# Moving four low-part subtractions to GpSimd, and a sum of the input's blocks behind the last attention unit

## The chip, the cores and the metric

The kernel runs on one core of a Trainium2 chip. Its engines are TensorE (PE: matmuls and transposes, with PEld for its weight loads), VectorE (DVE), ScalarE (ACT), GpSimd (POOL) and SyncE (SP), which issues the transfers. The metric is the time of one execution in microseconds of device time; the median of three runs stands for a kernel.

## The reference

One layer of a decoder over 512 positions of width 1024: a normalisation, one input projection, three attention branches (A block-sparse, B dilated in three groups, C sliding-window with sinks), each times a SiLU gate, a merge with sigmoid gates, and an output projection. Cut to what matters here:

```
hn = rms_norm(x, ln_g)
proj = hn @ w_in                       # q, k, v and silu inputs of A, B, C; gate logits
o_a, o_b, o_c = moba(...), dilated(...), swa_sink(...)
branches = stack([o_a * silu(ga), o_b * silu(gb), o_c * silu(gc)])
br = einsum('bsiw,iwd->bsid', branches, w_branch)
gates = sigmoid(gate_logits.reshape(b, s, 3, 1024))
merged = sum(gates * br, axis=2)
x = x + merged @ w_out
```

## The kernel before

**Precision.** Every large product is made of three: each operand is split into a high part of reduced precision and a low part, what is left of it. A weight tile w of 128 x 1024 is loaded by DMA; ScalarE casts it to whi (`split_hi`, L135); wlo = w − whi is a subtraction on VectorE or on GpSimd (`split_lo`, L140). In `load_w` (from L153) a counter sends every `every`-th of these to GpSimd and the others to VectorE, so `every=1` means all on GpSimd, and 1000 none. The same `split_lo` makes the low parts of softmax weights (ptlo), of row factors (ws) and of branches (bp) on VectorE.

**Stages.** Attention runs in ten units in turn, A0, W0, R0, Z0, A1, W1, R1, Z1, C0 and C1: A is branch A, W, R and Z are the three groups of branch B, and C0 and C1 are the two halves of branch C, four heads each. In a C unit, TensorE makes scores (L723 and L724), VectorE's row operation adds the bias and takes the row's extremum (`softmax_rows`, L584; it reads the scores from PSUM), ScalarE takes the exponential (L585), TensorE transposes (L731) and multiplies by the values (L610). When a unit ends, its row sums are inverted (L988 to L991 for C; L1018 to L1024 for B, where three groups are merged), and `spread` turns the factors into a row layout: a cast (L820), a subtraction ws (L140), transposes on TensorE (L827), a copy (L829), and a product that broadcasts them (L835), by which VectorE multiplies the output (L992, L1028).

**Filler.** The gates behind attention are a list of jobs. Jobs 0 and 1 ("raw", the SiLU inputs of B and A) are plain products of hn with weight tiles (L281 to L283); TensorE does them between the steps of C0 and C1, where it would wait for row operations. Their eight weight tiles are w_5105 to w_5147 (steps of 6) in the order's numbering. Job 2 ("gl", the first sigmoid gate, tiles w_5506 to w_5524) is plain too. From job 3 on the products use seven block products in place of eight, for which the input's blocks have to be added and subtracted first: `fast_x`, whose sums xf (L325) and differences (L339 to L346) run on VectorE. Behind C1 follow, for each gate, a load of the weights, sums of the weights' blocks, and the products.

**What sets the order.** Each engine works through a fixed order of its own. The kernel is traced in program order, and a scheduler with a model of the timeline then places each instruction; `tc.issue_after(x)` keeps what is issued within it behind instruction x. `fast_x()` was called without one: its inputs, the parts xhi and xlo of hn, are ready early, and each of its sums could go into any gap of VectorE once its buffer was free.

Of the kernel before, what the change touches and what calls it, by code (L numbers as in the profile page):

```python
# [12 lines left out]
ALU = mybir.AluOpType  # L13
# [7 lines left out]
KT = 8  # L21
# [82 lines left out]
def body(tc, x, ln_g, w_in, qk_g, sinks, w_branch, w_out, rel_bias, c_ident, c_onehot, c_mask, c_expand, out):  # L104
    nc = tc.nc
    V, A, G, T = nc.vector, nc.scalar, nc.gpsimd, nc.tensor
# [7 lines left out]
    with top:  # L114
# [18 lines left out]
        def split_hi(dst, src, eng=A):  # L133
            if eng is A:
                A.copy(dst, src)  # L135
            else:
                eng.tensor_copy(dst, src)  # L137

        def split_lo(dst, src, hi, eng=V):
            eng.tensor_tensor(dst, src, hi.bitcast(F32), ALU.subtract)  # L140
# [12 lines left out]
        def load_w(pieces, kts, early=False, every=LOEVERY):  # L153


            ncol = sum(n for n, _ in pieces)
            per = 1024 // ncol
            his, los = [], []
            for k0 in range(0, kts, per):
                w = wp.tile([128, per, ncol], F32, name="w32", tag="w32", bufs=LBUFS)  # L160
                o = 0
                for n, src in pieces:
                    nc.sync.dma_start(w[:, :, o : o + n], src(k0, k0 + per))
                    o += n
                hi = wp.tile([128, per, ncol], F32R, name="whi", tag="whi")
                lo = wp.tile([128, per, ncol], F32R, name="wlo", tag="wlo")
                nw[0] += 1
                split_hi(hi, w, V if early and nw[0] % 2 else A)
                split_lo(lo, w, hi, G if nw[0] % (2 if early else every) == 0 else V)
                his.append(hi)  # L170
                los.append(lo)
            return (lambda k: his[k // per][:, k % per]), (lambda k: los[k // per][:, k % per])

        def win_piece(c, n):
            return (n, lambda k0, k1: win[:, k0:k1, c : c + n])
# [100 lines left out]
        def gate_cols(w, c, psum):  # L276

            whi, wlo = w
            for k in range(KT):
                a = whi(k)[:, c : c + 128]  # L280
                T.matmul(psum, a, xhi[:, k, :], start=(k == 0), stop=False)  # L281
                T.matmul(psum, a, xlo[:, k, :], start=False, stop=False)  # L282
                T.matmul(psum, wlo(k)[:, c : c + 128], xhi[:, k, :], start=False, stop=(k == KT - 1))  # L283
                yield
# [32 lines left out]
        def fast_x():  # L317

            def quarter(k, j):
                ks, js = slice(4 * k, 4 * k + 4), slice(256 * j, 256 * j + 256)  # L320
                return xhi[:, ks, js], xlo[:, ks, js]

            def full(dst, k, j, eng):
                h, l = quarter(k, j)
                eng.tensor_tensor(dst, h.bitcast(F32), l.bitcast(F32), ALU.add)  # L325

            def parts(w, nm, eng):
                hi = gp.tile([128, 4, 256], F32R, name=nm + "h", tag=nm + "h", bufs=1)
                lo = gp.tile([128, 4, 256], F32R, name=nm + "l", tag=nm + "l", bufs=1)
                split_hi(hi, w)  # L330
                split_lo(lo, w, hi, eng)
                return hi, lo

            X, Y = (qkv.tile([128, 4, 256], F32, name="xf", tag="qlo") for _ in range(2))
            Z = gp.tile([128, 4, 256], F32, name="xf", tag="sm", bufs=1)
            full(X, 0, 1, V)
            full(Y, 0, 0, V)
            full(Z, 1, 1, V)
            V.tensor_tensor(Y, X, Y, ALU.subtract)  # L339
            t1 = parts(Y, "t1", V)  # L340
            V.tensor_tensor(X, Z, X, ALU.subtract)
            t3 = quarter(0, 1)
            V.tensor_tensor(Z, Z, Y, ALU.subtract)
            t2 = parts(Z, "t2", V)
            full(Y, 1, 0, V)
            V.tensor_tensor(Y, Y, Z, ALU.subtract)  # L346
            t4 = parts(Y, "t4", V)
            split_hi(t3[0], X)
            split_lo(t3[1], X, t3[0])
            return [quarter(0, 0), t1, t2, quarter(1, 0), t3, t4, quarter(1, 1)]  # L350
# [62 lines left out]
        def job_load(n):  # L413
            if n >= len(jobs):
                return None
            ty, u, v = jobs[n]
            if ty in ("raw", "gl"):
                c0 = v if ty == "raw" else GL + v * D + u * 512
                if n < PLAIN:
                    return load_w([win_piece(c0, 512)], KT, every=2)  # L420
                return fast_weights(lambda i, k: win[:, 4 * k : 4 * k + 4, c0 + 256 * i : c0 + 256 * i + 256])
            if ty == "br":
                return load_w([(512, lambda k0, k1: wbr[v, :, k0:k1, u * 512 : u * 512 + 512])], 4, every=1000)
            return load_w([(1024, lambda k0, k1: wou[:, k0:k1, :])], KT, every=1000)
# [3 lines left out]
        def raw_tile(br, hf):  # L428
            raws[br, hf] = qkv.tile([128, 2, S], F32, name="graw", tag=tags_raw[br, hf])
            return raws[br, hf]  # L430
# [14 lines left out]
        with att:  # L445
# [132 lines left out]
                v = tl[:, c0 : c0 + 128]  # L578
                return bass.AP(v.tensor, v.offset, [list(v.ap[0]), [step, n], [1, 128]])

            last_exp = [None]

            def softmax_rows(lg, sc, bt, init, mcol, lcol):
                V.tensor_tensor_reduce(lg, sc, bt, 1.0, init, ALU.add, ALU.min, mcol)  # L584
                last_exp[0] = A.activation(lg, lg, AF.Exp, bias=mcol, scale=-1.0, accum_out=lcol)  # L585

            def take_transposed(pend, tr):
# [453 lines left out]
        def slot(nm, tag, dt=F32R):  # L1041
            if tag[0] == "t":
                return gp.tile([128, 2, S], dt, name=nm, tag=tag, bufs=1)
            return qkv.tile([128, 2, S], dt, name=nm, tag=tag, **({"bufs": ORAWS} if tag == "oraw" else {}))
# [20 lines left out]
        xs = None  # L1065
# [12 lines left out]
        for n in range(2, len(jobs) - 1):  # L1078
            ty, dh, i = jobs[n]
            if n == PLAIN:  # L1080
                xs = fast_x()
            w, wnext = wnext, job_load(n + 1)
            if ty == "raw":
                fast_cols(w, xs, [raw_tile(dh, hf) for hf in range(2)], keep)
            elif ty == "gl":
                br = "ABC"[i]
                if dh == 0:
                    silu(br)
                sgs = [gp.tile([128, 2, S], F32, name="gsg", tag="sg") for _ in range(2)]
                if n < PLAIN:  # L1090
                    for dc in range(4):
                        pj = ps.tile([128, 512], F32, name="pj", tag="pj")
                        for _ in gate_cols(w, dc * 128, pj):
                            pass
                        A.activation(sgs[dc // 2][:, dc % 2], pj, AF.Sigmoid)
                else:
                    fast_cols(w, xs, sgs, gate)
            else:
                br = "ABC"[i]
                for dc in range(4):  # L1100
                    tg = ("pj", "sc", "tr", "po")[dc]
                    po = gsc[0][:, 1] if tg == "sc" else ps.tile([128, 512], F32, name="po", tag=tg)
                    for k in range(4):
                        a = w[0](k)[:, dc * 128 : dc * 128 + 128]
                        bh, bl = bhi[i, k // 2][:, k % 2], blo[i, k // 2][:, k % 2]
                        T.matmul(po, a, bh, start=(k == 0), stop=False)  # L1106
                        T.matmul(po, a, bl, start=False, stop=False)  # L1107
                        T.matmul(po, w[1](k)[:, dc * 128 : dc * 128 + 128], bh, start=False, stop=(k == 3))  # L1108
                    q = dh * 2 + dc // 2
                    sg = sgs[dc // 2][:, dc % 2]  # L1110
                    if br == ORDER[0]:
                        if q not in mg:
                            mg[q] = slot("mg", ("khi", "qlo")[dh], F32)
                        V.tensor_tensor(mg[q][:, dc % 2], po, sg, ALU.mult)
                    else:
                        V.tensor_tensor(sg, po, sg, ALU.mult)
                        V.tensor_tensor(mg[q][:, dc % 2], mg[q][:, dc % 2], sg, ALU.add)
                    if br == ORDER[2]:
                        if q not in mhi:
                            mhi[q], mlo[q] = slot("mh", tags_m[q * 2]), slot("ml", tags_m[q * 2 + 1])  # L1120
                        split_hi(mhi[q][:, dc % 2], mg[q][:, dc % 2])
                        split_lo(mlo[q][:, dc % 2], mg[q][:, dc % 2], mhi[q][:, dc % 2])
# [59 lines left out]
```

## Time and profile before

| | us |
|---|---|
| median of three runs | 795.5 |
| the three runs | 794.04, 795.5, 798.69 |
| the profiled execution | 795.95 |
| its span | 794.1 |
| PE busy | 770.3 |
| VectorE busy | 494.8 |
| ScalarE busy | 412.0 |
| GpSimd busy | 223.8 |

The profile is of one execution; the span reaches from its first to its last instruction, and 1.85 us of the execution's own time lie around it. Times in rows are counted from the span's start. A row's bracket gives the idle time of the engine ahead of an instruction and the instruction whose end released it. The granted clock of TensorE is 1.00 at 2.4 GHz and 0.50 at 1.2 GHz; a value between is a mean over the stretch.

### The profile page before, as it was taken

What the parts mean: (1) busy time and instruction counts of PE and PEld (TensorE: products, weight loads), DVE (VectorE), ACT (ScalarE), POOL (GpSimd) and SP (SyncE); (2) the same over time, 40 slices, a digit from 0 to 9 for tenths busy, and PEclk for the clock granted to TensorE, in tenths of its full rate; (3) what the DMA queues carried; (4) which work ended last, traced back from release to release, by engine and by line L of the source; (5) the groups of instructions that cost most, each with busy time, mean ns of one, the idle gap of its engine ahead of it and who ended that gap; (6) DMA issues with size and microseconds to landing.
All of it is one profiled execution on the core that took longest, in us unless ns stands there. A gap on an engine that the chain in (4) does not pass through costs nothing.

```text
span 794.1 us, 12665 instructions
## 1 busy us (share of the span) xinstructions
PE 770.3 (97%) x4727; PEld 657.7 (83%) x4727; DVE 494.8 (62%) x1067; ACT 412.0 (52%) x914; POOL 223.8 (28%) x139
## 2 busy tenths in 40 slices
PE   7999999999999989999999999899999999999998
PEld 4887788788878878878887877687899999999886
DVE  6453653546447565354646876658999797987512
ACT  5544563766475446376747646465455344445300
POOL 3694333442753552435173241100000000000000
PEclk9999999999999989999999999999999999999999
DMA  9443433361343043425233021514054233436302
GB/s 291 129 129 96 118 99 110 103 200 37 107 113 80 21 126 99 127 84 185 71 106 109 18 87 46 160 25 148 27 160 150 89 91 123 140 99 210 109 1 106
DMA packets 67329, 85.99 MB, mean 108 GB/s; under 512 B 4899, under 2 KB 53155, under 8 KB 67268
## 3 DMA queue, kind: packets, MB, share of 16 engines
q1 hardware_dynamic: 67268, 85.19, 35.4%
q8 instruction: 37, 0.61, 0.3%
q14 instruction: 24, 0.20, 0.1%
HBM read 75.67 MB, written 9.50 MB: 107 GB/s over the span
## 4 chain that ended last, share of the span: by engine, by line
PE 89%; DVE 4%; ACT 2%; POOL 1%; issue 1%; DMA 1%; SPq 0%; POOLq 0%; DVEq 0%; ACTq 0%
PE pj L500 13%; PE pj L501 12%; PE pj L502 12%; PE fc L361 11%; PE acc L1136 6%; PE fsc L361 4%; PE po L610 3%; PE pj L281 3%; PE pj L282 3%; PE pj L283 3%; PE sc L660 2%; PE tr L680 2%; PE po L1106 2%; PE po L1107 2%; PE po L1108 2%; PE tr L557 2%
## 5 line engine op out<-in xcount | busy, mean ns | idle before, releaser
L500 PE MATMUL pj<-whi,xhi 128*128 128x512 f32 (+1 forms) x576 | 203.5, 354 | 2.3 <-DVE whi L137 0.8
L501 PE MATMUL pj<-wlo,xhi 128*128 128x512 f32 (+1 forms) x576 | 196.9, 343 | 0.0
L502 PE MATMUL pj<-whi,xlo 128*128 128x512 f32 (+1 forms) x576 | 195.7, 341 | 0.0
L140 POOL TENSOR_TENSOR wlo<-w,whi 128x1024 fp32r<-128x1024 f32 x58 | 142.0, 2466 | 138.5 <-ACT whi L135 133.1
L135 ACT CAST whi<-w 128x1024 fp32r<-128x1024 f32 x108 | 112.9, 1050 | 85.2 <-PE fsc L361 18.8
L500 PEld LDWEIGHTS pj<-whi,xhi 128*128 128x128 f32 x576 | 109.5, 190 | 18.7 <-issue 2.3
L502 PEld LDWEIGHTS pj<-whi,xlo 128*128 128x128 f32 x576 | 109.5, 190 | 12.5
L501 PEld LDWEIGHTS pj<-wlo,xhi 128*128 128x128 f32 x576 | 109.8, 191 | 11.3 <-DVE wlo L140 0.4
L148 POOL TENSOR_TENSOR rr<-rv,mhalf 128x8 f32<-128x8 f32 (+2 forms) x40 | 62.0, 1552 | 143.7 <-DVE rv L146 140.4
L140 DVE TENSOR_TENSOR ptlo<-tr,pthi 128x128 fp32r<-128x128 f32 (+3 forms) x112 | 51.0, 459 | 59.2 <-ACT pthi L135 38.5
L140 DVE TENSOR_TENSOR wlo<-w,whi 128x1024 fp32r<-128x1024 f32 x52 | 66.0, 1279 | 23.0 <-ACT whi L135 23.0
L135 ACT CAST pthi<-tr 128x128 fp32r<-128x128 f32 (+3 forms) x112 | 44.5, 402 | 60.4 <-PE tr L680 25.4
L527 DVE TENSOR_TENSOR qn<-qn,rr 128x512 f32<-128x512 f32 (+1 forms) x36 | 34.6, 961 | 21.5 <-POOL rr L148 21.5
L516 DVE TENSOR_REDUCE ss<-sq 128x8 f32<-128x512 f32 (+2 forms) x40 | 25.6, 641 | 31.1 <-ACT sq L514 30.5
L584 DVE CUSTOM_DVE_ANT_0 lg<-sc,bt 128x128 f32<-128x128 f32 (+2 forms) x96 | 28.4, 337 | 19.6 <-PE sc L660 9.8
L361 PE MATMUL fc<-xhi,wlo 128*128 128x256 f32 x144 | 40.2, 279 | 0.0
L361 PE MATMUL fc<-xlo,whi 128*128 128x256 f32 x144 | 40.2, 279 | 0.0
L361 PE MATMUL fc<-xhi,whi 128*128 128x256 f32 x144 | 40.2, 279 | 0.0
L281 PE MATMUL pj<-xhi,whi 128*128 128x512 f32 x96 | 40.1, 418 | 0.0
L585 ACT ACTIVATE lg<-lg,sm 128x128 f32<-128x128 f32 (+1 forms) x80 | 32.7, 410 | 12.1 <-DVE sm L584 12.0
L282 PE MATMUL pj<-xlo,whi 128*128 128x512 f32 x96 | 38.3, 399 | 0.0
L283 PE MATMUL pj<-xhi,wlo 128*128 128x512 f32 x96 | 38.1, 397 | 0.0
(262 smaller groups left out, 1700.3 us busy)
## 6 DMA issues: line engine op xcount, KB each, us to landing
w<-in_w_in SPq DMA_DIRECT2D x54, 512.0 KB, 4.5
w<-in_w_in SPq DMA_DIRECT2D x72, 256.0 KB, 3.1
w<-in_w_branch SPq DMA_DIRECT2D x12, 512.0 KB, 3.2
vscr<-vn SPq DMA_DIRECT2D x16, 256.0 KB, 2.8
w<-in_w_out SPq DMA_DIRECT2D x8, 512.0 KB, 3.4
osp<-oraw SPq DMA_DIRECT2D x6, 512.0 KB, 2.6
oback<-osp SPq DMA_DIRECT2D x6, 512.0 KB
xt<-in_x SPq DMA_DIRECT2D x4, 512.0 KB, 5.7
```

Source lines behind the costliest of these rows:

```text
L135: A.copy(dst, src)
L140: eng.tensor_tensor(dst, src, hi.bitcast(F32), ALU.subtract)
L148: pows.append(G.tensor_tensor(r, v, mhalf[:, :n], ALU.pow))
L281: T.matmul(psum, a, xhi[:, k, :], start=(k == 0), stop=False)
L282: T.matmul(psum, a, xlo[:, k, :], start=False, stop=False)
L283: T.matmul(psum, wlo(k)[:, c : c + 128], xhi[:, k, :], start=False, stop=(k == KT - 1))
L361: T.matmul(psum[:, c], w[:, k, cs], x_[:, k, :], start=(first and c == 0 and k == 0 and q == 0), stop=(c == 1 and k == 3 and q == 2), skip ...
L500: T.matmul(pj[:, :ncol], xh, whi(k), start=(k == 0), stop=False)
L501: T.matmul(pj[:, :ncol], xh, wlo(k), start=False, stop=False)
L502: pe = T.matmul(pj[:, :ncol], xl, whi(k), start=False, stop=(k == KT - 1))
L527: V.tensor_tensor(q3[:, :nq], q3[:, :nq], r[:, :nq].unsqueeze(2).broadcast_to([128, nq, 64]), ALU.mult)
L1136: T.matmul(acc[t * 2 + e], part[k // 2][:, k % 2, tsl], wo[q](k)[:, es], start=(k == 0 and q == 0 and part is mhi), stop=(k == KT - 1 and ...
```

## The change

Two edits, in `job_load` and around the call of `fast_x`. The raw jobs' low parts, of which every second one was VectorE's, are all GpSimd's now: tiles w_5105, w_5117, w_5129 and w_5141 move. The first of `fast_x`'s instructions may only come behind the last row operation that was issued, which is C1's last; `softmax_rows` keeps that instruction for it.

```diff
@@ job_load
             if ty in ("raw", "gl"):
                 c0 = v if ty == "raw" else GL + v * D + u * 512
                 if n < PLAIN:
-                    return load_w([win_piece(c0, 512)], KT, every=2)
+                    return load_w([win_piece(c0, 512)], KT, every=1 if ty == "raw" else 2)
...
@@ softmax_rows
-            last_exp = [None]
+            last_exp, last_row = [None], [None]
 
             def softmax_rows(lg, sc, bt, init, mcol, lcol):
-                V.tensor_tensor_reduce(lg, sc, bt, 1.0, init, ALU.add, ALU.min, mcol)
+                last_row[0] = V.tensor_tensor_reduce(lg, sc, bt, 1.0, init, ALU.add, ALU.min, mcol)
...
@@ the loop over the jobs
             if n == PLAIN:
-                xs = fast_x()
+                with tc.issue_after(last_row[0].ins):
+                    xs = fast_x()
```

No instruction is added or taken away. The orders that come out differ as follows; in the order's rows, "ISA lg,sl" of L584 is the row operation, sl the row sums, ex the sink's exponent, w_... a weight tile, and x3 three instructions in a row.

VectorE at the end of unit C0, before:

```order
L140 TENSOR_TENSOR wlo<-w_5141,whi 128x1024
L140 TENSOR_TENSOR ptlo<-tr,pthi 128x2x128
L584 ISA lg,sl<-sc,bt,nsk 128x256
L584 ISA sl 128x1
L325 TENSOR_TENSOR xf<-xhi,xlo 128x1024
L988 TENSOR_TENSOR ex<-sl,nsk 128x16
L584 ISA lg,sl<-sc,bt,nsk 128x128
L584 ISA sl 128x1
L140 TENSOR_TENSOR wlo<-w_5506,whi 128x1024
L990 TENSOR_TENSOR sl<-sl,ex 128x4x4
```

and with the change:

```order
L988 TENSOR_TENSOR ex<-sl,nsk 128x16
L584 ISA lg,sl<-sc,bt,nsk 128x128
L584 ISA sl 128x1
L990 TENSOR_TENSOR sl<-sl,ex 128x4x4
L991 RECIPROCAL sl<-sl 128x4x4
L820 CAST ws<-sl 128x4x4
L140 TENSOR_TENSOR ws<-sl,ws 128x4x4
L584 ISA lg,sl<-sc,bt,nsk 128x256
L584 ISA sl 128x1
L140 TENSOR_TENSOR wlo<-w_5506,whi 128x1024
```

The subtraction of w_5141 and the sum xf are gone from here, and the reciprocal, the cast and the subtraction ws stand directly behind L990, ahead of two row operations and of the subtraction of w_5506. On TensorE the transposes of ws (L827) move at the same place; the piece of the difference reads:

```order
+L827 MATMUL trs<-revr,ws 64x128 x4
 L610 MATMUL po<-pthi,vhi 128x256
 L723 MATMUL sc<-khi,qhi 128x256
 L724 MATMUL sc<-klo,qhi 128x256
-L723 MATMUL sc<-khi,qhi 128x256
-L724 MATMUL sc<-klo,qhi 128x256
-L827 MATMUL trs<-revr,ws 64x128 x4
```

They come ahead of a value product and of one pair of score products, where they stood behind two pairs. At the merge of branch B, some 40 us earlier, VectorE's order before is:

```order
L140 TENSOR_TENSOR wlo<-w_5129,whi 128x1024
L1022 RECIPROCAL den<-den 128x16
L480 TENSOR_TENSOR qs<-qb,qs 128x4x64
L527 TENSOR_TENSOR qb<-qb,rr_5047 128x256
L568 SCALAR_TENSOR_TENSOR klo<-tr,gqk,khi 128x2x128
L1024 TENSOR_TENSOR sm<-sm,den 128x4x4 x3
L479 CAST qs<-qb 128x4x64
```

and with the change:

```order
L1022 RECIPROCAL den<-den 128x16
L480 TENSOR_TENSOR qs<-qb,qs 128x4x64
L1024 TENSOR_TENSOR sm<-sm,den 128x4x4 x3
L527 TENSOR_TENSOR qb<-qb,rr_5047 128x256
L820 CAST ws<-sm 128x4x4 x2
L568 SCALAR_TENSOR_TENSOR klo<-tr,gqk,khi 128x2x128
```

The subtraction of w_5129 is gone, and the three L1024, which make the groups' factors, stand ahead of L527 (keys and queries of C) and L568 (a low part of keys for TensorE).

## Rows read from the trace of the kernel before

**Rows 1.** The page's first and second parts: busy time of each engine in us, its share of the span and its instructions, and the granted clock of TensorE in 40 equal slices of the span, in tenths.
```profile
PE 770.3 (97%) x4727; PEld 657.7 (83%) x4727; DVE 494.8 (62%) x1067; ACT 412.0 (52%) x914; POOL 223.8 (28%) x139
...
PEclk9999999999999989999999999999999999999999
```

**Rows 2.** Busy time of each engine in four stretches: from and to, length, busy us of each engine (instructions), the granted clock, the share of the DMA engines and their GB/s.
```profile
500.00:520.00 20.00, 17.99 (x94) 15.11 (x95) 11.94 (x30) 9.24 (x29) 2.31 (x1) 0.91 0.45 137
502.00:506.00 4.00, 3.60 (x16) 3.13 (x17) 1.75 (x5) 0.87 (x3) 0.31 (x1) 0.60 0.44 139
520.00:540.00 20.00, 20.00 (x109) 17.08 (x108) 13.32 (x26) 14.78 (x33) 2.83 (x1) 1.00 0.18 51
560.00:580.00 20.00, 20.00 (x124) 17.78 (x123) 19.30 (x19) 11.17 (x13) 0.00 (x0) 1.00 0.11 31
```

**Rows 3.** What TensorE waited for over the whole span: its operation and line, the engine, tile and line waited for, us in total, times, longest.
```profile
PE sc L723 <- DVE sl L584: 2.0, 3, 1.2
...
PE trs L827 <- DVE ws L140: 1.9, 1, 1.9
...
PE po L1106 <- DVE oraw L992: 0.5, 1, 0.5
```

**Rows 4.** TensorE's timeline at C0's end: start, duration, engine, line, operation, out<-in, shape and count, and in brackets the idle time ahead of it and what ended it.
```profile
493.74 0.38 PE L723 MATMUL sc<-khi,qhi 128*128 128x256 f32 x1 [0.27 <-DVE sl L584]
...
497.02 0.38 PE L723 MATMUL sc<-khi,qhi 128*128 128x256 f32 x1 [1.18 <-DVE sl L584]
...
499.97 0.39 PE L723 MATMUL sc<-khi,qhi 128*128 128x256 f32 x1 [0.58 <-DVE sl L584]
...
502.40 0.63 PE L827 MATMUL trs<-revr,ws 128*64 128x128 f32 x4 [1.92 <-DVE ws L140]
...
503.11 0.78 PE L281 MATMUL pj<-xhi,whi 128*128 128x512 f32 x1
...
505.33 0.40 PE L283 MATMUL pj<-xhi,wlo 128*128 128x512 f32 x1
```

**Rows 5.** VectorE's timeline at C0's end.
```profile
491.72 1.23 DVE L140 TENSOR_TENSOR wlo<-w,whi 128x1024 fp32r<-128x1024 f32 x1 [0.51 <-ACT whi L135]
...
493.20 0.48 DVE L584 CUSTOM_DVE_ANT_0 lg<-sc,bt,nsk 128x256 f32<-128x256 f32 x1
...
493.60 3.01 DVE L325 TENSOR_TENSOR xf<-xhi,xlo 128x1024 f32<-128x1024 f32 x1
...
496.62 0.34 DVE L584 CUSTOM_DVE_ANT_0 lg<-sc,bt,nsk 128x128 f32<-128x128 f32 x1
...
500.04 2.30 DVE L140 TENSOR_TENSOR ws<-sl,ws 128x16 fp32r<-128x16 f32 x1
```

**Rows 6.** The sums xf in the view of that tile: line, engine, operation, count, shortest, median and longest in ns, first and last start in us.
```profile
L325 DVE TENSOR_TENSOR xf<-xhi,xlo x4: 1216/1221/3012, 493.6 to 560.6; 128x1024 f32<-128x1024 f32 x4
```

**Rows 7.** GpSimd's timeline at C0's end.
```profile
493.14 2.39 POOL L140 TENSOR_TENSOR wlo<-w,whi 128x1024 fp32r<-128x1024 f32 x1 [19.27 <-ACT whi L135]
499.96 2.35 POOL L140 TENSOR_TENSOR wlo<-w,whi 128x1024 fp32r<-128x1024 f32 x1 [4.43 <-ACT whi L135]
```

**Rows 8.** The page's fifth part, the subtractions that make the weights' low parts: busy us and mean ns of one on GpSimd and on VectorE.
```profile
L140 POOL TENSOR_TENSOR wlo<-w,whi 128x1024 fp32r<-128x1024 f32 x58 | 142.0, 2466 | 138.5 <-ACT whi L135 133.1
...
L140 DVE TENSOR_TENSOR wlo<-w,whi 128x1024 fp32r<-128x1024 f32 x52 | 66.0, 1279 | 23.0 <-ACT whi L135 23.0
```

**Rows 9.** Timelines of VectorE and then of GpSimd at the merge of branch B.
```profile
455.69 1.22 DVE L140 TENSOR_TENSOR wlo<-w,whi 128x1024 fp32r<-128x1024 f32 x1
...
457.60 0.47 DVE L568 SCALAR_TENSOR_TENSOR klo<-tr,gqk,khi 128x256 fp32r<-128x256 f32 x1
457.99 2.41 DVE L1024 TENSOR_TENSOR sm<-sm,den 128x16 f32<-128x16 f32 x3
...
457.80 2.41 POOL L140 TENSOR_TENSOR wlo<-w,whi 128x1024 fp32r<-128x1024 f32 x1 [1.82 <-ACT whi L135]
```

**Rows 10.** TensorE's timeline at the merge of branch B.
```profile
462.08 0.46 PE L483 MATMUL tr<-revr,qs 128*128 128x128 f32 x4
```

**Rows 11.** Timelines of VectorE and then of GpSimd at the end of unit Z1.
```profile
428.66 2.54 DVE L140 TENSOR_TENSOR wlo<-w,whi 128x1024 fp32r<-128x1024 f32 x1 [1.83 <-ACT whi L135]
431.21 0.29 DVE L584 CUSTOM_DVE_ANT_0 lg<-sc,bt 128x128 f32<-128x128 f32 x1
...
427.76 5.68 POOL L140 TENSOR_TENSOR wlo<-w,whi 128x1024 fp32r<-128x1024 f32 x2 [6.27 <-ACT whi L135]
```

**Rows 12.** Timelines of VectorE, GpSimd and TensorE behind C1's last row operation.
```profile
535.07 2.06 DVE L988 TENSOR_TENSOR ex<-sl,nsk 128x16 f32<-128x16 f32 x1
...
545.78 1.23 DVE L140 TENSOR_TENSOR bp<-oback,bp 128x1024 fp32r<-128x1024 f32 x1
...
548.72 1.23 DVE L140 TENSOR_TENSOR bp<-oback,bp 128x1024 fp32r<-128x1024 f32 x1 [1.11 <-ACT bp L135]
...
554.00 1.29 DVE L992 TENSOR_TENSOR oraw<-oraw,pb 128x512 f32<-128x512 f32 x2 [2.62 <-PE pb L835]
...
534.26 2.83 POOL L140 TENSOR_TENSOR wlo<-w,whi 128x1024 fp32r<-128x1024 f32 x1 [31.95 <-ACT whi L135]
...
548.42 0.45 PE L1107 MATMUL fsc<-bp,whi 128*128 128x512 f32 x1
```

## The prediction

> **What bounds the kernel now.** I read the page first. TensorE (PE) is busy 770.3 of the 794.1 us span, VectorE 62%, GpSimd 28% [rows 1]. So only what PE waits for can be won, and what a slower clock costs. The digits of the clock show one 8 near 278 us, which the change does not touch [rows 1]; the table by stretches is finer: from 500 to 520 PE is busy for 17.99 of 20 us at a granted clock of 0.91, and 502 to 506 stands at 0.60 [rows 2]. The view of PE's waits names whom it waited for there: the score products of L723 lost 2.0 us in three waits for VectorE's row operation L584, and the transposes of L827 lost 1.9 us in one wait for the subtraction that makes ws [rows 3]. All four lie between 493 and 503 us, at the end of unit C0. In PE's timeline they read 1.18 us ahead of 497.02, 0.58 ahead of 499.97 and 1.92 ahead of 502.40; what is left of the 2.0 is a short first one of 0.27 [rows 4]. Behind the longest one the products take 0.63 to 0.78 us, where from 505.33 on they take 0.40: the lower level of the clock, 1.2 in place of 2.4 GHz [rows 4]. From 502.40 to 505.33 are 2.93 us, and half of it, about 1.45, is the price of the clock.
>
> Why VectorE was late is the next view. The sum xf at 493.60 took 3.01 us [rows 5], where the median of the four sums is 1.22 [rows 6], and the tiny ws at 500.04 took 2.30 [rows 5]. Both lie beside a GpSimd subtraction of 2.4 us and outlast it little or not: 493.14 + 2.39 = 495.53, and then 1.0 of the xf's own work; 499.96 + 2.35 = 502.31, against 502.34 [rows 5, 7]. The row operation at 493.20 (0.48 us, scores in PSUM) ran beside the same GpSimd instruction undisturbed [rows 5]. I read it so: a VectorE operation with both inputs in SBUF is held until GpSimd's subtraction has ended.
>
> **The change part by part.** Removed from VectorE: four subtractions of 128x1024, 1.28 us each by their group, 5.1 together. GpSimd gets them at 2.47 each, 9.9 us [rows 8]. Moved: one xf of 1.22 us, from behind C0's to behind C1's last row operation. Nothing else is added; the scheduler reorders around it. Four places follow.
>
> *C0's end (492 to 506), the gain.* The subtraction at 491.72 goes (1.23), the xf at 493.60 goes (3.01), and the row operation of 493.20 moves up to about 492.5. GpSimd now does w_5141 from 491.7 to 494.1 and w_5147 right behind, to about 496.6. L988, with two SBUF inputs, is held until 494.1. I assume that it gets in between the two, since xf and ws each ran as soon as one subtraction had ended. The next row operation, at 496.62 before [rows 5], then comes at about 494.2. L990 is held until 496.6; L991, L820 and ws, now next in the order, end at about 497.3 in place of 502.34. The GpSimd subtraction that held ws cannot meet it any more: its cast stands on ScalarE behind an exp that needs a row operation queued behind ws. PE has L827 four rows earlier, and I estimate 0.35 us of waiting left there (ws at 497.3 and its handover, PE there at about 497.3). So 2.0 + 1.92 of idle time and 1.45 of clock, less 0.35: 5.0 us. Lower bound 3.5: if L988 is not let in between, the row operation stays at 496.6 with its wait of 1.18, and about 0.3 more is lost behind it. Upper bound 5.35: no wait left at L827.
>
> *Branch B's merge (455 to 464), a loss.* VectorE's subtraction at 455.69 goes, but GpSimd now does w_5129 (about 456.0 to 458.4) and w_5135 (to 460.8) in a row, where it had one at 457.80. The three L1024 stood behind L527 and L568 and were held once, 2.41 us from 457.99; now they stand ahead of those, and are held by both, to about 461.2 [rows 9]. Behind them on VectorE queue L527, L820 and L568. L568, at 457.60 before [rows 9], comes at about 462.2, and ws a microsecond later than before. PE's order puts the reversals L483 that wait for it (462.08 before [rows 10]) and L827 ahead of two groups of filler products, so PE waits about 0.9 and 0.4 us; I estimate that 0.5 of it comes back behind, where the fillers now stand. Loss 0.8; bounds 0 (VectorE is let in earlier) and 2.8 (1.3 of waits, nothing back, and 1.45 of clock).
>
> *Z1's end (425 to 438).* Two VectorE subtractions go, one of which took 2.54; GpSimd does four in a row in place of two (5.68 us), until about 435.2. VectorE's next work, row operations from 431.21, needs PE's scores and reads PSUM [rows 11], as the one that ran undisturbed at 493.20 did. Cost nothing; without that cover one held operation would cost what ws took, 2.30.
>
> *Behind C1's last row operation (532 to 556).* VectorE does two xf there in place of one. GpSimd's subtraction at 534.26 (2.83 us) holds the second, so L988, held until 537.13 before, comes at about 538.6, and with it the table load, the SiLU products and the split of bp: 1.0 to 1.55 us later. PE's first use of a bp that this delays lies at 548.42 (L1107), and the bp was ready at 545.78 + 1.23 = 547.01: 1.4 us to spare [rows 12], so 0.2 of waiting. Against it, L835 moves ahead of some L1108 products, and the wait of 0.5 us for L992 [rows 3] goes. Together −0.35; bounds −0.55 and +0.6. VectorE's idle 1.11 and 2.62 us ahead of 548.72 and 554.00 take up the added 1.22 [rows 12]. From 560 to 580 PE was busy 20.00 of 20 us beside VectorE's 19.30 [rows 2]; there only neighbours are swapped: 0.
>
> The sum: −5.0 + 0.8 + 0 − 0.35 = −4.55 us. The profiled execution took 795.95 us (span 794.1), so it gives 791.4. That execution lies 0.45 above the median of the three runs, 795.5; on that scale **790.9 us**.
>
> A rule of the Trainium skill speaks against the change. SBUF — State Buffer, section Who interferes with whom, says that a VectorE instruction with two SBUF inputs contends with a GpSimd instruction that reads SBUF, by an exclusive lock on which the second blocks fully. The trace agrees (2.30 us for the ws). By that rule alone 5.1 us of VectorE's work would be exchanged for up to 9.9 us in which it may be blocked, 4.8 lost; my sum counts it only where PE waits for what is held.
>
> **Rivals.** (A) *The move to GpSimd buys nothing; only xf's does.* L988 is held through both subtractions, so the row operation stays at 496.6: −3.5 + 0.8 − 0.35 = −3.05, 792.4 us. For it: GpSimd did the two at 427.76 as one block of 5.68 us [rows 11]. Against it: xf got in at 495.5. Beside it stands the Trainium skill, Perfetto Trace Analysis, section Optimizing Scalar/DVE Operations: since the two engines share a port, offloading between them might not help. No run here has shown such a move yet.
>
> (B) *Slower: pairs on GpSimd stretch and stall PE until its clock falls.* The pair at 427.76 took 5.68, not twice 2.4 [rows 11]. So stretched, it holds branch B's merge 0.9 longer: waits of 0.9 + 0.4 + 0.9 = 2.2, longer than the wait of 1.92 behind which the clock stood low [rows 4], so +1.45: 3.65 there. At C0's end the wait of 1.18 becomes 2.1 and the slow clock comes with it, so only 0.27 + 0.58 + 1.92 − 0.9 = 1.9 is won. With 0.6 behind C1: +2.35, 797.8 us, up to 800 if the clock falls there too. It decides where PE's waits near 462 are as long as that of 502.40. Against it: that pair ran beside a VectorE subtraction of 2.54 us, and here none is left.
>
> (C) *The wait only moves.* PE comes 5 us sooner to C1, where its scores follow row operations one by one; if these set the pace up to 532, the idle time comes back and only the clock's part is won: −1.45 + 0.8 − 0.35 = −1.0, 794.5 us. Against it: PE was busy 20.00 from 520 to 540 [rows 2].
>
> **How the numbers follow.** A measurement of this kernel can tell about 0.5%, 4.0 us, from no change, so faster means below 791.5. My forecast (chance 0.60; own range 789.6, by −5.35 + 0 − 0.55, to 792.3, by a merge that costs 2.2) lies just beyond it: 0.45 faster, 0.15 same. A 0.20: 0.05 and 0.15. B 0.10: half same, half slower. C 0.10: 0.08 same, 0.02 slower. Sum: faster 0.50, same 0.43, slower 0.07. The range goes from 788.8 (the best case, and 0.8 for the median, which three runs put between 794.04 and 798.69) over A and C to 795.6, and leaves out B and a little at the low end.
>
> **What would show it.** Right: near 497 no wait at L827 over 1 us and no product of 0.63 us behind it; ws ends 5 us earlier; every xf but the held second one takes 1.22; L1024 is held from 456 to 461. A: the row operation of 496.62 stays there. B: products of 0.6 us near 462. C: new waits of L723 behind 505. Wrong altogether: VectorE isn't held by the new GpSimd work (then 0.8 less), or PE's 20.00 of 20 us from 560 on falls because VectorE's 19.30 had no room.

## The result, and the profile after

The kernel with both edits takes 790.57 us, the median of six runs (790.05 to 791.71), against 795.46 for the kernel before, six runs too (794.04 to 798.89). The ratio is 0.9949, 95% interval 0.9932 to 0.9966: 4.9 us, 0.5%, faster. The profiled execution took 790.23 us with a span of 788.4, 5.7 less than that of before.

The page's busy times, and what is left in the view of PE's waits for VectorE at the two places where C0 and branch B end:

```profile
PE 768.5 (97%) x4727; PEld 656.4 (83%) x4727; DVE 491.6 (62%) x1063; ACT 411.3 (52%) x914; POOL 232.5 (29%) x143
...
PE tr L483 <- DVE klo L568: 0.3, 1, 0.3
PE trs L827 <- DVE ws L140: 0.3, 1, 0.3
```

The wait of L723 for the row operation, 2.0 us before, has left the list, and that of L827 fell from 1.9 to 0.3 [rows 3]; GpSimd is busy 8.7 us more [rows 1]. The stretches that showed the slower clock read now, in the columns of [rows 2]:

```profile
500.00:520.00 20.00, 19.66 (x113) 16.83 (x112) 11.35 (x36) 11.58 (x35) 1.97 (x1) 1.00 0.46 146
502.00:506.00 4.00, 3.66 (x21) 2.94 (x20) 3.13 (x9) 2.58 (x9) 0.00 (x0) 1.00 0.74 247
560.00:580.00 20.00, 20.00 (x148) 18.90 (x146) 18.74 (x19) 12.49 (x15) 0.00 (x0) 1.00 0.36 112
```

The clock is 1.00 where it was 0.91 and 0.60, and from 560 on PE is still busy for 20.00 of 20 us. Timelines of PE, VectorE and GpSimd at C0's end:

```profile
495.24 0.37 PE L723 MATMUL sc<-khi,qhi 128*128 128x256 f32 x1
...
497.50 0.43 PE L827 MATMUL trs<-revr,ws 128*64 128x128 f32 x4 [0.26 <-DVE ws L140]
...
498.79 0.48 PE L281 MATMUL pj<-xhi,whi 128*128 128x512 f32 x1
...
492.66 0.48 DVE L584 CUSTOM_DVE_ANT_0 lg<-sc,bt,nsk 128x256 f32<-128x256 f32 x1
...
493.19 1.19 DVE L988 TENSOR_TENSOR ex<-sl,nsk 128x16 f32<-128x16 f32 x1
494.30 0.34 DVE L584 CUSTOM_DVE_ANT_0 lg<-sc,bt,nsk 128x128 f32<-128x128 f32 x1
...
494.66 2.08 DVE L990 TENSOR_TENSOR sl<-sl,ex 128x16 f32<-128x16 f32 x1
...
497.27 0.17 DVE L140 TENSOR_TENSOR ws<-sl,ws 128x16 fp32r<-128x16 f32 x1
...
491.94 2.41 POOL L140 TENSOR_TENSOR wlo<-w,whi 128x1024 fp32r<-128x1024 f32 x1 [17.90 <-ACT whi L135]
```

These answer to [rows 4, 5 and 7]. GpSimd does its two subtractions without a pause, 491.94 to 496.71. VectorE's L988 is held 1.19 us, until the first ends, and gets in; the row operation runs at 494.30, where it stood at 496.62; L990 is held until the second ends. Then ws takes 0.17 us in place of 2.30 and ends at 497.44. PE waits 0.26 us at L827, and the products behind run at 0.48 and less, not 0.78.

At the merge of branch B (VectorE, GpSimd, PE):

```profile
455.94 2.39 DVE L1024 TENSOR_TENSOR sm<-sm,den 128x16 f32<-128x16 f32 x1
...
461.14 0.47 DVE L568 SCALAR_TENSOR_TENSOR klo<-tr,gqk,khi 128x256 fp32r<-128x256 f32 x1
...
455.75 2.55 POOL L140 TENSOR_TENSOR wlo<-w,whi 128x1024 fp32r<-128x1024 f32 x1
...
461.67 0.36 PE L483 MATMUL tr<-revr,qs 128*128 128x128 f32 x2 [0.33 <-DVE klo L568]
```

The three L1024 are held through both GpSimd subtractions, 4.78 us in place of 2.41 [rows 9], and PE waits 0.33 us for L568's key part. Behind C1's last row operation:

```profile
528.79 4.58 DVE L325 TENSOR_TENSOR xf<-xhi,xlo 128x1024 f32<-128x1024 f32 x2
...
533.62 0.16 DVE L988 TENSOR_TENSOR ex<-sl,nsk 128x16 f32<-128x16 f32 x1
...
549.57 0.69 DVE L992 TENSOR_TENSOR oraw<-oraw,pb 128x512 f32<-128x512 f32 x1 [1.53 <-PE pb L835]
...
529.46 2.83 POOL L140 TENSOR_TENSOR wlo<-w,whi 128x1024 fp32r<-128x1024 f32 x1 [27.49 <-ACT whi L135]
```

The second xf is held by GpSimd's subtraction (4.58 us for the two), and L988 ends at 533.78, 6.5 us behind the start of the last row operation (527.24), where it was 5.1 before (537.13 and 532.05) [rows 12]. PE is busy for 26.00 of 26 us from 530 to 556: it waits neither for bp nor for L992.

Where the time went is read from the same instruction in both traces, in PE's timeline (behind the call of `fast_x` the line numbers of the changed kernel are one higher, so its L1107 is the L1106 of before). Of before:

```profile
456.11 0.40 PE L281 MATMUL pj<-xhi,whi 128*128 128x512 f32 x1
...
492.04 0.28 PE L723 MATMUL sc<-khi,qlo 128*128 128x256 f32 x1
...
531.62 0.28 PE L723 MATMUL sc<-khi,qlo 128*128 128x256 f32 x1
...
547.72 0.40 PE L1106 MATMUL fsc<-bp,whi 128*128 128x512 f32 x1
```

And with the change:

```profile
455.91 0.40 PE L281 MATMUL pj<-xhi,whi 128*128 128x512 f32 x1
...
492.22 0.28 PE L723 MATMUL sc<-khi,qlo 128*128 128x256 f32 x1
...
526.81 0.28 PE L723 MATMUL sc<-khi,qlo 128*128 128x256 f32 x1
...
542.89 0.40 PE L1107 MATMUL fsc<-bp,whi 128*128 128x512 f32 x1
```

The first filler product behind Z1 comes 0.20 us earlier, though nothing ahead of it has been reordered but the subtractions at Z1's end, so this isn't put down to the change; a score product of C0 0.18 later, so the merge cost 0.38; one at C1's end 4.81 earlier, so C0's end with C1 behind it won 4.99; the first product of the merge with branch B's weights 4.83 earlier; the span's end 5.7 earlier, so the rest won 0.87, of which 0.5 is the wait for L992.

### The profile page after: what moved, and what is told of

The parts are those of the page before. It is cut to its first block, busy times and chain, and to the rows that moved or that the text cites. A ratio compares the mean times of both kernels' runs of the same rounds, so it can differ in the third digit from the quotient of the medians.

```text
span 788.4 us, 12663 instructions
## 1 busy us (share of the span) xinstructions
PE 768.5 (97%) x4727; PEld 656.4 (83%) x4727; DVE 491.6 (62%) x1063; ACT 411.3 (52%) x914; POOL 232.5 (29%) x143
## 4 chain that ended last, share of the span: by engine, by line
PE 90%; DVE 4%; ACT 2%; POOL 1%; issue 1%; DMA 1%; SPq 0%; POOLq 0%; DVEq 0%; ACTq 0%
PE pj L500 13%; PE pj L501 12%; PE pj L502 12%; PE fc L361 11%; PE acc L1137 6%; PE fsc L361 4%; PE po L610 3%; PE sc L660 3%; PE pj L281 2%; PE pj L283 2%; PE pj L282 2%; PE tr L680 2%; PE po L1107 2%; PE po L1108 2%; PE po L1109 2%; PE tr L557 2%
## 5 line engine op out<-in xcount | busy, mean ns | idle before, releaser
L500 PE MATMUL pj<-whi,xhi 128*128 128x512 f32 (+1 forms) x576 | 203.3, 354 | 2.1 <-DVE whi L137 0.8
L502 PE MATMUL pj<-whi,xlo 128*128 128x512 f32 (+1 forms) x576 | 195.8, 341 | 0.0
L140 POOL TENSOR_TENSOR wlo<-w,whi 128x1024 fp32r<-128x1024 f32 x62 | 150.7, 2450 | 126.5 <-ACT whi L135 125.1
L500 PEld LDWEIGHTS pj<-whi,xhi 128*128 128x128 f32 x576 | 109.2, 190 | 18.5 <-issue 2.6
L502 PEld LDWEIGHTS pj<-whi,xlo 128*128 128x128 f32 x576 | 109.4, 190 | 12.5
L140 DVE TENSOR_TENSOR wlo<-w,whi 128x1024 fp32r<-128x1024 f32 x48 | 59.9, 1257 | 18.7 <-ACT whi L135 18.7
L527 DVE TENSOR_TENSOR qn<-qn,rr 128x512 f32<-128x512 f32 (+1 forms) x36 | 34.6, 962 | 21.6 <-POOL rr L148 21.6
L584 DVE CUSTOM_DVE_ANT_0 lg<-sc,bt 128x128 f32<-128x128 f32 (+2 forms) x96 | 28.4, 337 | 27.0 <-PE sc L660 9.7
```

The costliest lines, as they stand in the source:

```text
L500: T.matmul(pj[:, :ncol], xh, whi(k), start=(k == 0), stop=False)
L502: pe = T.matmul(pj[:, :ncol], xl, whi(k), start=False, stop=(k == KT - 1))
L527: V.tensor_tensor(q3[:, :nq], q3[:, :nq], r[:, :nq].unsqueeze(2).broadcast_to([128, nq, 64]), ALU.mult)
```

## The experiments

Every ratio below is to the kernel before, run on the same chip (its median there 794.1 to 794.8 us). My theory was that of the prediction: what costs is that a VectorE operation is held while GpSimd subtracts, and only where PE then waits. The rivals were that the edits each bring a part, that GpSimd's work as such costs, and that the new order, not the end of the holds, made the gain.

**One edit alone.** First the subtractions without the sums:

```diff
-                    return load_w([win_piece(c0, 512)], KT, every=2)
+                    return load_w([win_piece(c0, 512)], KT, every=1 if ty == "raw" else 2)
```

> Only the first edit: the four subtractions go to GpSimd, the sum xf stays behind C0's last row operation. If the holds set the time (my theory), xf is held by GpSimd's first subtraction there and itself holds up the second, L988 is held by the second, so the row operation of 496.62 comes at about 497.9: PE waits at L723 by 2 us or more, ws still meets the next GpSimd subtraction, the clock falls as before, and branch B's merge costs its 0.4. Then 795.5 to 797.5 us, no gain at all. If the two edits add up, each with a part of the gain (rival), about 793.

Measured: 797.34 us, ratio 1.0043 (1.0026 to 1.0060): slower than before, at the upper end of what the theory gave. VectorE and PE at C0's end:

```profile
493.65 2.37 DVE L325 TENSOR_TENSOR xf<-xhi,xlo 128x1024 f32<-128x1024 f32 x1
495.95 2.31 DVE L988 TENSOR_TENSOR ex<-sl,nsk 128x16 f32<-128x16 f32 x1
...
498.58 0.58 PE L723 MATMUL sc<-khi,qhi 128*128 128x256 f32 x1 [2.50 <-DVE sl L584]
...
505.32 0.64 PE L827 MATMUL trs<-revr,ws 128*64 128x128 f32 x4 [1.85 <-DVE ws L140]
```

The xf is held by the first subtraction (2.37 us), L988 behind it by the second (2.31), so PE waits 2.50 us at L723, and 1.85 once more at L827 for the ws, which still meets w_5512. The edits do not add up.

Then the sums without the subtractions:

```diff
...
             if n == PLAIN:
-                xs = fast_x()
+                with tc.issue_after(last_row[0].ins):
+                    xs = fast_x()
```

> Only the second edit: the sums behind C1's last row operation, the raw low parts shared out as before. My theory: with xf gone, L988 is held by one GpSimd subtraction only until about 495.5, the row operation comes a microsecond earlier than before, and ws, now ahead in the order, no longer meets a GpSimd subtraction: no half-clock stretch behind C0. 4.7 us won there and nothing lost at the merge: 790 to 791, the whole gain, so that moving the subtractions adds nothing. If both edits are needed, 793 or more.

Measured: 789.73 us, ratio 0.9940 (0.9923 to 0.9958), at least as good as both edits. PE and then VectorE at C0's end:

```profile
491.50 0.28 PE L723 MATMUL sc<-khi,qlo 128*128 128x256 f32 x1
...
493.18 1.85 DVE L988 TENSOR_TENSOR ex<-sl,nsk 128x16 f32<-128x16 f32 x1
494.95 0.34 DVE L584 CUSTOM_DVE_ANT_0 lg<-sc,bt,nsk 128x128 f32<-128x128 f32 x1
...
496.01 0.18 DVE L140 TENSOR_TENSOR ws<-sl,ws 128x16 fp32r<-128x16 f32 x1
```

One GpSimd subtraction holds L988 for 1.85 us; the row operation comes at 494.95, which is early enough for PE, and ws is through at 496.19. Counted from the same score product (491.50 here, 492.22 with both edits), that is half a microsecond before the kernel with both edits. Counted likewise from 492.04 in the kernel before, the row operation comes 1.13 us sooner, about what xf took behind its own hold: with xf gone L988 is held in its place, so here the edit takes away xf's own work and not the hold. The whole gain is the second edit's.

**No GpSimd work at the place.** All raw low parts on VectorE, with the sums moved:

```diff
-                    return load_w([win_piece(c0, 512)], KT, every=1 if ty == "raw" else 2)
+                    return load_w([win_piece(c0, 512)], KT, every=1000 if ty == "raw" else 2)
```

> The second edit, and all eight raw low parts on VectorE, none on GpSimd. If GpSimd's work as such is what costs (rival), this is the fastest of all, below 790. My theory: L988 and L1024 are not held any more and the wait of 1.18 goes, but ws stands behind the subtraction of w_5506 and two row operations again in this order and meets GpSimd's w_5512, 2 us held, PE waiting about 2 us at L827 and its clock at the lower level behind: 793 to 794.5.

Measured: 792.67 us, ratio 0.9976 (0.9965 to 0.9987). VectorE, then PE:

```profile
496.51 2.21 DVE L140 TENSOR_TENSOR ws<-sl,ws 128x16 fp32r<-128x16 f32 x1
...
498.78 0.51 PE L827 MATMUL trs<-revr,ws 128*64 128x128 f32 x4 [1.83 <-DVE ws L140]
```

ws is held 2.21 us by the one subtraction that GpSimd still has there, PE waits 1.83, and the products behind take 0.63 to 0.78 us. That this one hold is what it lacks was tried by giving VectorE w_5512 as well, the 64th weight tile in `load_w`'s count:

```diff
-                split_lo(lo, w, hi, G if nw[0] % (2 if early else every) == 0 else V)
+                split_lo(lo, w, hi, G if nw[0] % (2 if early else every) == 0 and nw[0] not in (64,) else V)
```

> The second edit, all eight raw low parts on VectorE, and w_5512 too, so that GpSimd does no subtraction from 435 to the end of C1 but the last. My theory: the hold of ws by w_5512 was all that this lacked; the wait of 1.8 at L827 and the clock's 1.45 go, 789 to 789.5. If VectorE's own five added subtractions of 1.2 us set the pace at C0's end (rival), 792 or more.

Measured: 790.65 us, ratio 0.9947 (0.9926 to 0.9969). The theory holds in kind: the wait at L827 is gone. It was too low by 1 us or more: three waits of L723 for row operations (1.3 us in all) stay, as in the run above; why they do was not tried. GpSimd's share of this work is neither good nor bad in itself.

The same line in the kernel before, with neither edit:

> The kernel before, with neither edit, and only w_5512's subtraction, the one that ran beside ws at 500, given to VectorE; xf stays behind C0's last row operation. My theory: ws is not held, the wait of 1.92 at L827 and the clock's part go, those of L723 (2.0 us) stay: 791.5 to 793. If the whole 5 us hang on xf (rival), 795.

Measured: 792.48 us, ratio 0.9973 (0.9955 to 0.9990). The wait of L827 is gone, and of L723 this one is left, with two smaller:

```profile
496.54 0.39 PE L723 MATMUL sc<-khi,qhi 128*128 128x256 f32 x1 [1.20 <-DVE sl L584]
```

So the two delays at C0's end, of the row operation behind xf and L988 and of ws, are each worth some 2 us (this run and the one with all raw parts on VectorE), and the second edit ends both: at the row operation it takes away xf's own work, and ws is through before GpSimd's next subtraction starts. What the hold of xf alone is worth was not tried: no run keeps xf there and takes GpSimd's subtraction away.

**More GpSimd work, same order.** With both edits, the subtraction of w_5147 (the 62nd tile) is done twice, which changes no order on PE or VectorE:

```diff
-                split_lo(lo, w, hi, G if nw[0] % (2 if early else every) == 0 else V)
+                for _ in range(2 if nw[0] == 62 else 1): split_lo(lo, w, hi, G if nw[0] % (2 if early else every) == 0 else V)
```

> The kernel with both edits, and GpSimd does the subtraction of w_5147 twice, the second writing the same values again; the orders of PE and VectorE stay as they are. The work added is GpSimd's alone, 2.4 us at C0's end. My theory: L990, held until 496.7 with the change, is held until 499.1, ws ends near 499.7, PE waits some 2.6 us at L827 in place of 0.3, and the clock falls behind it: 2.4 + 1.45 = 3.8 us, 794.4. If the new order made the gain and the holds do not matter (rival), 790.6.

Measured: 793.81 us, ratio 0.9991 (0.9977 to 1.0005): 3.3 us of the gain are lost to 2.4 us of GpSimd work whose result is not needed. GpSimd, VectorE, PE and the clock there:

```profile
490.02 7.21 POOL L140 TENSOR_TENSOR wlo<-w,whi 128x1024 fp32r<-128x1024 f32 x3 [17.89 <-ACT whi L135]
...
495.15 2.10 DVE L820 CAST ws<-sl 128x16 fp32r<-128x16 f32 x1
...
497.52 0.44 PE L827 MATMUL trs<-revr,ws 128*64 128x128 f32 x4 [2.20 <-DVE ws L140]
...
496.00:504.00 8.00, 6.30 (x38) 5.27 (x38) 7.36 (x17) 4.67 (x13) 3.64 (x2) 1.00 0.48 145
```

The hold, not the order, makes the time. What was held is not what I had said: L990 got in behind the second subtraction, and the third held the cast of ws (L820), whose only input is in SBUF. And in this execution the clock did not fall behind the wait of 2.20 us; it is the fastest of the twelve, which reach from 790.36 us at a mean clock of 0.996 to 795.82 at 0.987. PE's wait grew by 1.94 us (0.26 to 2.20); the other 1.4 of the 3.3 us may be the clock's in the other eleven, of which there is no trace.

The same with w_5135 (the 60th tile), at branch B's merge:

> The kernel with both edits, and GpSimd does the subtraction of w_5135 twice, so that three stand in a row at branch B's merge; orders as with the change. My theory: if VectorE's three small L1024 get in between one by one, the third is in by the time the third subtraction starts, and then at most L527 or L820 is held: 0 to 2.4 us of PE waiting at L483, with the clock 790.6 to 794.4. If the hold lasts as long as GpSimd is busy (rival), L1024 takes 7.2 us and PE waits 2.7: 794.4.

Measured: 792.72 us, ratio 0.9976 (0.9964 to 0.9988). VectorE, then PE:

```profile
463.39 2.58 DVE L527 TENSOR_TENSOR qb<-qb,rr 128x256 f32<-128x256 f32 x1
...
466.76 0.39 PE L723 MATMUL sc<-khi,qhi 128*128 128x256 f32 x1 [1.99 <-DVE sl L584]
```

My expectation was wrong in where the third subtraction falls: GpSimd did it behind the reciprocal root rr, at 463.33, and it held L527 (2.58 in place of 0.43 us), so that a row operation of C0 came late and PE waited 1.99. The price, some 2 us, lies within the range that I gave for another place.

**Less at the merge.** With both edits, w_5129 (the 59th tile) stays on VectorE:

```diff
-                split_lo(lo, w, hi, G if nw[0] % (2 if early else every) == 0 else V)
+                split_lo(lo, w, hi, G if nw[0] % (2 if early else every) == 0 and nw[0] not in (59,) else V)
```

> Both edits, but w_5129's subtraction is left on VectorE, so that GpSimd does one in place of two at branch B's merge; the orders there are those of before, the rest is as with the change. My theory: the 0.4 us that PE lost at the merge come back, 790.2, and L1024 is held 2.4 in place of 4.8 us. If the merge costs nothing, 790.6; a gain of 0.4 is hardly to be told in the time, so the waits at the merge decide.

Measured: 790.74 us, ratio 0.9952 (0.9935 to 0.9969), not to be told from both edits. L1024 takes 2.42 us again, and the wait of 0.33 at L483 is gone. In halves (the two slices z of each raw tile):

```diff
-                split_lo(lo, w, hi, G if nw[0] % (2 if early else every) == 0 else V)
+                for z in ((slice(0, per // 2), slice(per // 2, per)) if 55 <= nw[0] <= 62 else (slice(0, per),)): split_lo(lo[:, z], w[:, z], hi[:, z], G if nw[0] % (2 if early else every) == 0 else V)
```

> The kernel with both edits; the eight raw subtractions on GpSimd are each issued as two of 128x512, with the orders of PE and VectorE as they are. My theory: GpSimd holds the port for one instruction, and a waiting VectorE operation gets in between two. With halves of 1.2 us, L988 is held by less than 1 us, L990 by 1.2 at most, and the three L1024 get in one per half, 3.6 in place of 4.8 us; the waits of 0.3 at L483 and L827 go: 0.5 less, 790.0. If the hold lasts until GpSimd's queue runs dry (rival), L1024 still takes 4.8 us and the time stays at 790.6.

Measured: 789.83 us, ratio 0.9938 (0.9914 to 0.9963); the intervals overlap with both edits. VectorE at the merge:

```profile
454.62 2.56 DVE L1024 TENSOR_TENSOR sm<-sm,den 128x16 f32<-128x16 f32 x3
...
457.44 1.34 DVE L820 CAST ws<-sm 128x16 fp32r<-128x16 f32 x2
```

L1024 takes 2.56 in place of 4.78 us, while GpSimd is busy there for 5.43 without a pause: VectorE gets in between two GpSimd instructions. The next half then holds the casts L820 (1.34 us for two).

**Where the same thing costs elsewhere.** PE's longest wait for VectorE, 2.4 us at L557, lies near 289 us, where GpSimd's reciprocal root stands behind the subtraction of w_3407 (the 40th tile). With the second edit alone, this tile goes to VectorE:

```diff
-                split_lo(lo, w, hi, G if nw[0] % (2 if early else every) == 0 else V)
+                split_lo(lo, w, hi, G if nw[0] % (2 if early else every) == 0 and nw[0] not in (40,) else V)
```

> The second edit alone, and one more subtraction, that of w_3407 in the middle of the kernel, given from GpSimd to VectorE. There GpSimd's reciprocal root rr stands behind this subtraction (2.39 us at 283.43 with the change), and PE waits 2.4 us at L557 for what needs rr, with the clock at the lower level behind. My theory: VectorE does it in 1.2 us where it has room, rr comes 2.4 us earlier, the wait and the clock's part go: 3 to 4 us, 786 to 787. If VectorE's added work lies on the way of the same wait, 789 to 790.

Measured: 786.96 us, ratio 0.9901 (0.9881 to 0.9921), the fastest here, and faster than both kernels. VectorE, PE and the clock, and then the clock with the second edit alone:

```profile
280.16 3.40 DVE L140 TENSOR_TENSOR wlo<-w,whi 128x1024 fp32r<-128x1024 f32 x1
...
285.13 0.36 PE L500 MATMUL pj<-whi,xhi 128*128 128x256 f32 x1 [1.45 <-DVE vlo L140]
...
288.00:296.00 8.00, 6.49 (x50) 5.33 (x49) 4.97 (x16) 5.00 (x15) 0.00 (x0) 1.00 0.53 177
```

```profile
288.00:296.00 8.00, 5.82 (x33) 4.61 (x34) 5.42 (x15) 3.78 (x12) 0.62 (x1) 0.79 0.28 108
```

VectorE's subtraction is itself held (3.40 us beside GpSimd's pair), rr comes only 0.95 us earlier than with the second edit alone (284.80 against 285.75), not 2.4, and a wait of 1.45 appears at L500; but L557's shrinks from 2.31 to 0.24, and the clock stays up, where it stood at 0.79 with the second edit alone (0.57 with both edits, 0.64 before). Against the second edit alone the ratio is 0.4% lower, some 3 us. These two waits make 0.6 of it; the rest was not parted between the clock and the order behind, which changes too. With w_3400 on VectorE too:

```diff
-                split_lo(lo, w, hi, G if nw[0] % (2 if early else every) == 0 and nw[0] not in (40,) else V)
+                split_lo(lo, w, hi, G if nw[0] % (2 if early else every) == 0 and nw[0] not in (39, 40) else V)
```

> The second edit alone, with w_3400 and w_3407 both on VectorE. With w_3407 alone there, VectorE's subtraction was itself held 3.4 us beside GpSimd's pair, and 1.4 us of waiting moved to L500, which waits for vlo behind it. With one GpSimd subtraction left there, my theory has VectorE held by 2.4 at most and that wait gone: 1.4 us less, 785.5. If two more on VectorE are too many there, 787 or more.

Measured: 786.98 us, ratio 0.9904 (0.9877 to 0.9930): no further gain. VectorE's subtraction took 2.30 us in place of 3.40, as expected, but the waits of L500 only fell from 1.6 to 1.3 us in all; this expectation was a miss.

## Why the prediction was right, and where it was off

**What bounded the kernel** held: PE's waits at C0's end and the clock behind them were what could be won. With the change both are gone but for 0.26 us. That 790.9 lies so close to 790.57 is in part luck: in the profiled executions 5.7 us were won, not 4.55, since the merge cost 0.4 less, the part behind C1 brought 0.5 more, and 0.2 came from ahead of both, all the same way; the medians lie only 4.9 apart.

**C0's end.** The mechanism came out step by step: GpSimd from 491.94 to 496.71 (predicted 491.7 to 496.6), L988 let in after the first subtraction, the row operation at 494.30 (about 494.2), ws done at 497.44 (about 497.3), 0.26 us of waiting at L827 (0.35). Won with C1 behind it: 4.99 us of 5.0. Rival A is out in its mechanism, since the row operation did not stay at 496.6, and C too: no waits of L723 came back behind 505.

**What my sum did not see** is which edit the 5.0 belong to. I walked through both at once and counted the subtraction of w_5141 leaving VectorE among the causes. Alone, the first edit costs 0.4% and the second brings 0.6%; together they bring no more than the second by itself. Rival A's heading, that the move to GpSimd buys nothing, was right where its price and its reason were wrong. The rule of the Trainium skill that I set beside it (Perfetto Trace Analysis, section Optimizing Scalar/DVE Operations: offloading between VectorE and GpSimd might not help) agrees with these runs, 1.0043 for the move alone.

**Branch B's merge** was mis-sized: 0.8 predicted, 0.38 measured. L1024 was held through both subtractions, as said, but those ended 0.1 us earlier than I had put them, and L568 followed at 461.14, not 462.2; PE waited 0.33 at L483 and hardly at L827, not 0.9 and 0.4. I had added the operations queued behind L1024 at more than they take.

**Z1's end** cost nothing that the trace shows: GpSimd did four subtractions in 9.38 us, and the row operations beside them took 0.28 and 0.29 us as before.

**Behind C1's last row operation** the order of events was as said: the second xf held, L988 late by 1.5 us, no wait for L992. The 0.2 us of waiting for bp did not come. Won were 0.87 us by the profiled executions, where I had 0.35; 0.3 of that lies behind 556 without a wait that the trace names, and stays open.

**The clock's 1.45 us** is the term that I would now write with a chance. It was lost in the profiled execution of before, and not in that of the doubled w_5147, behind a longer wait; its median leaves room for such a loss in its other executions.

B was out: no wait at L483 or L827 near 462 came near 1.9 us. Its pairs did not stretch: 4.94 and 4.77 us. Only with xf in their way (5.69 us for the pair in the kernel with the first edit alone) did they, and that kernel is the slower one.

## What to carry to other kernels

Where GpSimd works on SBUF, look up what VectorE has to do in those microseconds and who waits for that; a tiny operation on the way to TensorE can cost the whole of GpSimd's instruction. Moving a large operation that nobody waits for out of such a place can be worth more than moving work to an idle engine, and two edits that look like one idea should be run apart. Shorter GpSimd instructions let VectorE in sooner, though here the time did not show it.

## What the runs showed of the hardware that was not expected

An operation with a single input in SBUF is held too: the cast L820 of 128x16 took 2.10 us beside GpSimd's third subtraction, where it takes 0.17. The prediction had put this on operations with two SBUF inputs, though the trace of before had an exception: L146, which scales 128x8 sums and whose median is 0.17 us, took 1.65 beside a pair of GpSimd's subtractions.

```profile
280.56 1.65 DVE L146 TENSOR_SCALAR rv<-ss 128x8 f32<-128x8 f32 x1
...
276.97 5.21 POOL L140 TENSOR_TENSOR wlo<-w,whi 128x1024 fp32r<-128x1024 f32 x2
```

The Trainium skill (SBUF — State Buffer, section Who interferes with whom) says that a copy or a cast can contend in a two-port mode, and the held cast agrees, though no row shows its mode. In the run with w_5147 doubled the reciprocal L991 (0.25 us at 494.87, as GpSimd went on) and the row operations were not held.

The clock does not answer to the length of a wait alone. PE's granted clock fell behind idle times of 1.83, 1.92 and 2.50 us in three kernels, and stayed at 1.00 behind 2.20 and 1.99 in two others, in one execution of each. It also falls in some executions at places that no edit touched, as these stretches of the kernel with the change and of the kernel before show:

```profile
88.00:96.00 8.00, 6.91 (x40) 5.45 (x41) 5.54 (x17) 4.70 (x15) 0.00 (x0) 0.79 0.09 22
```

```profile
88.00:96.00 8.00, 6.05 (x44) 4.57 (x43) 5.60 (x17) 5.63 (x16) 0.00 (x0) 1.00 0.04 7
```

PE's order is the same in both up to there. The changed kernel was 0.67 us ahead at its L502 of 16.45 (17.12 before) and only 0.07 at that of 100.81 (100.88), so this stretch took 0.6 us. Runs of one kernel spread by more: 24 of the kernel before on one chip reach from 791.88 us at a mean clock of 0.995 to 797.25 at 0.989, which is why the medians, not the two spans, give the result.
